# Moving the DRAM additions of a seven-product matmul: a pause under the first blocks of w_up, a denser run from the sixth block on

## The chip, the cores and the metric

One core of a Trainium2 chip runs the kernel. The metric is the device time of one execution in microseconds. Before the change three runs gave a median of 1739.53 us (1737.74 to 1740.78).

## What is computed

One decoder block on 256 tokens of width 2048, float32: a norm, one wide input projection, two branches (a gated linear recurrence and a dilated attention), their merge, and then a feed-forward part with a causal convolution of width 3. The change touches only how the weights of that feed-forward part are prepared:

```python
def conv_ffn(u, w_up, conv_w, conv_b, w_down):
    hup = u @ w_up                       # 2048 -> 2 x 5632
    hc = lax.conv_general_dilated(hup, ...) + conv_b
    a, b = hc[..., :D_FF], hc[..., D_FF:]
    return (jax.nn.gelu(a) * b) @ w_down
...
h = h + conv_ffn(rmsnorm(h, norm2_g[l]), w_up[l], conv_w[l], conv_b[l], w_down[l])
```

## The kernel before, in words

All weights are streamed once, in the order in which TensorE needs them, as 300 units of 1 MB (128 partitions x 2048 floats). `load(u)` (line 290) brings a unit into one of three `raw` slots, from SP's queue. `split(u)` turns each float into a high and a low part that TensorE can multiply fast: ScalarE (ACT) copies the high part (line 380 for plain units), VectorE (DVE) subtracts to get the low part (line 381). A product is then three matmuls.

Units 0 to 131 are the input projection, 132 to 167 the merge and output projections, 168 to 299 the feed-forward part. That part runs in 11 blocks `b`, each with 8 units of `w_up`, and from block 1 on two or four units of `w_down` behind them; from block 3 on a block is 12 units. The results of a `w_down` piece are evicted by ACT to a staging tile (`dns`, line 1078) and added to `h` by an accumulating DMA from POOL's queue (line 1079); ACT, DVE and TensorE meanwhile work off the convolution of the block before (`hidden_side`, line 1043: the transposes into `ua..t`, `ub..t` at line 1028, the taps `..e` at line 1036, from the same ring of staging tiles).

In most `w_up` units (mode "S", 60 of 88) TensorE does a 2 x 2 block product with seven products in place of eight. For that four sums of the unit's weight blocks are needed. Two of them, q1 (the first block plus the fourth) and q2 (q1 plus the third), are made in DRAM long before. `add_blocks` (line 255) makes one step of that: it copies a weight block into a DRAM tile (SP, 256 KB) and adds another to it with an accumulating DMA (POOL, line 267, 256 KB), which gives q1 of the next S unit; and for the unit three steps back it copies q1 to a second tile (SP, line 266) and adds the third block (POOL), which gives q2. So a full call issues two DMAs on SP and two on POOL; the last three calls of all find no new unit and issue one each. The SP copies are ordered behind the latest load of a whole unit (`in_turn(loaded[-1])`).

An S unit is then loaded as three transfers: 768 KB of weights (line 297), q1 behind them (line 298), and q2 into a tile of its own (line 300). `split_s` splits q2 (`sg`), the four blocks (`sa`, `se`), forms two more sums on DVE (lines 354, 355) and splits those (`sf`), all at lines 327 and 328. A plain unit is one transfer of 1 MB (line 303).

`begin_unit(u)` (line 414) is the clock of the whole: before the matmuls of unit `u` it splits units up to `u + 2`, loads unit `u + 3`, runs some side work, and then calls `add_blocks` until `additions(u)` calls have been made. `additions` (line 137) is the schedule that the change rewrites; 60 S units and three trailing steps make 63 calls.

Of the kernel before, what the change touches and what calls it, by code (L numbers as in the profile page):

```python
# [130 lines left out]
MODES = stream_spec()[1]  # L131

DRAM_SUMS = sorted(u for u, mode in MODES.items() if mode == "S")
ADD_FROM, ADD_TO, ADD_LATE = 44, 166, 8


def additions(u):
    n = len(DRAM_SUMS) + 3
    if u <= ADD_TO:
        return max(0, (u - ADD_FROM) * (n - 12) // (ADD_TO - ADD_FROM))  # L140
    return min(n, n - 12 + (u - ADD_TO) // ADD_LATE)

# [49 lines left out]
def hybrid_block(ctx, tc, x_p, x_t, weights, g1, gf, params, c_rope, c_mask0, c_mask1, c_level, out):  # L194
# [219 lines left out]
    def begin_unit(u):  # L414
        for v in range(u, u + LOOKAHEAD + 1):
            split(v)
        load(u + LOOKAHEAD + 1)
        pump(SIDE_US)
        while added[0] < additions(u):
            add_blocks()  # L420
            added[0] += 1
# [742 lines left out]
```

## Time and profile before

| | |
|---|---|
| median of 3 runs | 1739.53 us |
| the profiled execution's own time | 1738.46 us |
| its span | 1736.7 us |
| TensorE busy | 1713.5 us |
| DVE busy | 1301.3 us |
| ACT busy | 1053.7 us |
| granted TensorE clock, mean | 0.998 |

The span runs from the first to the last instruction. "Busy" is the time in which an engine had at least one instruction under way. A wait row names the engine and tile that waited and the one that released it. "DMA share" is the mean busy share of the core's 16 DMA engines. `up4v`, `ub3t` and so on are tiles of block 4 and block 3.

### The profile page before, as it was taken

To read this page: it belongs to the slowest core of one execution; us is meant where nothing else is said; L and a number is where in the kernel's file an instruction comes from. 1 tells how busy PE (TensorE), PEld (TensorE's weight loads), DVE (VectorE), ACT (ScalarE), POOL (GpSimd) and SP (SyncE) were. 2 spreads that over 40 slices of the span, in tenths; PEclk is the share of its full clock that TensorE was granted. 3 is DMA by queue.
4 is the path that set the end of the run, shared out by engine and by line. 5 is a ranking of instruction groups with operands and counts; after the bars stand their busy time and mean duration, and the time that the engine had idled before them with its cause. 6 is when DMAs were issued, how large, how long until landed. Compare 5 with 4: busy or idle time off the path is not lost. (4 is left out here: it accounts for less than half of the span.)

```text
span 1736.7 us, 22219 instructions
## 1 busy us (share of the span) xinstructions
PE 1713.5 (99%) x8292; PEld 1428.7 (82%) x8292; DVE 1301.3 (75%) x1559; ACT 1053.7 (61%) x1436; POOL 140.5 (8%) x181
## 2 busy tenths in 40 slices
PE   9999999999999999999999999999999999999998
PEld 8888888888888888888888887787777878888886
DVE  7765575776858675444656688999889889889886
ACT  6444465555455554544445568877776777887773
POOL 0000000011111011011111100110110110110000
PEclk9999999999999999999999999999999999999999
DMA  7765634778778787889998977887787788787672
GB/s 279 232 207 201 232 145 160 229 230 242 229 247 243 225 257 224 259 271 289 293 272 249 274 231 249 277 254 249 210 286 258 229 279 269 217 263 262 204 263 97
DMA packets 98684, 416.19 MB, mean 240 GB/s; under 512 B 11936, under 2 KB 12192, under 8 KB 67152
## 3 DMA queue, kind: packets, MB, share of 16 engines
q1 hardware_dynamic: 73344, 365.22, 58.5%
q0 software_dynamic: 23936, 46.15, 16.3%
q10 hardware_dynamic: 1296, 3.41, 0.5%
q8 instruction: 65, 1.06, 0.2%
q14 instruction: 43, 0.35, 0.1%
HBM read 400.05 MB, written 65.01 MB: 268 GB/s over the span
## 5 line engine op out<-in xcount | busy, mean ns | idle before, releaser
L380 ACT ACTIVATE hl<-raw 128x1024 fp32r<-128x1024 f32 (+1 forms) x480 | 500.9, 1055 | 502.1 <-PE egp L539 79.1
L381 DVE TENSOR_TENSOR hl<-raw,hl 128x1024 fp32r<-128x1024 f32 (+1 forms) x480 | 579.2, 1218 | 292.2 <-ACT hl L380 290.5
L267 POOL DMA_DIRECT2D q<-weights x120 | 99.7, 901 | 1113.3 <-DMA q<-q 821.3
L537 PE MATMUL dn<-hl,ff 128*128 128x512 f32 x320 | 126.7, 399 | 0.2 <-DVE up2c L621 0.2
L539 PE MATMUL dn<-hl,ff 128*128 128x512 f32 x320 | 125.0, 391 | 0.0
L538 PE MATMUL dn<-hl,ff 128*128 128x512 f32 x320 | 124.7, 390 | 0.0
L537 PE MATMUL egp<-hl,xu 128*128 128x512 f32 x256 | 100.5, 393 | 0.0
L539 PE MATMUL egp<-hl,xu 128*128 128x512 f32 x256 | 99.8, 390 | 0.0
L538 PE MATMUL egp<-hl,xu 128*128 128x512 f32 x256 | 99.7, 389 | 0.0
L328 DVE TENSOR_TENSOR se<-raw,se 128x1024 fp32r<-128x1024 f32 x60 | 73.2, 1221 | 16.6 <-ACT se L327 16.5
L327 ACT ACTIVATE sf<-raw 128x1024 fp32r<-128x1024 f32 x60 | 64.0, 1067 | 30.7 <-DVE raw L355 30.2
L328 DVE TENSOR_TENSOR sa<-raw,sa 128x1024 fp32r<-128x1024 f32 x60 | 73.2, 1220 | 9.8 <-ACT sa L327 9.8
L328 DVE TENSOR_TENSOR sf<-raw,sf 128x1024 fp32r<-128x1024 f32 x60 | 73.3, 1222 | 8.4 <-ACT sf L327 8.2
L327 ACT ACTIVATE se<-raw 128x1024 fp32r<-128x1024 f32 x60 | 63.9, 1066 | 25.1 <-PE up L600 12.6
L539 PEld LDWEIGHTS dn<-hl,ff 128*128 128x128 f32 x320 | 60.1, 188 | 13.1
L537 PEld LDWEIGHTS dn<-hl,ff 128*128 128x128 f32 x320 | 60.1, 188 | 12.7 <-DVE up2c L621 0.6
L538 PEld LDWEIGHTS dn<-hl,ff 128*128 128x128 f32 x320 | 60.2, 188 | 11.6
L327 ACT ACTIVATE sa<-raw 128x1024 fp32r<-128x1024 f32 x60 | 63.7, 1061 | 8.6 <-PE dn L539 4.9
L450 PE MATMUL ak<-xu,hl 128*128 128x512 f32 x192 | 67.1, 394 | 0.0
L539 PEld LDWEIGHTS egp<-hl,xu 128*128 128x128 f32 x256 | 48.1, 188 | 9.9
L538 PEld LDWEIGHTS egp<-hl,xu 128*128 128x128 f32 x256 | 48.1, 188 | 9.7
L537 PEld LDWEIGHTS egp<-hl,xu 128*128 128x128 f32 x256 | 48.1, 188 | 9.7
(585 smaller groups left out, 4417.6 us busy)
## 6 DMA issues: line engine op xcount, KB each, us to landing
raw<-weights SPq DMA_DIRECT2D x238, 1024.0 KB, 5.4
raw<-weights SPq DMA_DIRECT2D x60, 768.0 KB, 5.8
q<-weights POOLq DMA_DIRECT2D x120, 256.0 KB, 7.4
q<-q SPq DMA_DIRECT2D x120, 256.0 KB, 5.1
q<-weights SPq DMA_DIRECT2D x60, 256.0 KB, 6.3
raw<-q SPq DMA_DIRECT2D x60, 256.0 KB, 6.1
h<-dns POOLq DMA_DIRECT2D x36, 256.0 KB, 6.2
h<-x_t ACTq DMA_DIRECT2D x4, 512.0 KB, 6.6
```

What stands on the lines that cost most here:

```text
L267: nc.gpsimd.dma_start(q, weights[u, :, i * 512 : (i + 1) * 512], accum_op=ALU.add)
L327: act.activation(hi, src, AF.Copy)
L328: vec.tensor_tensor(lo, src, hi.bitcast(F32), op=ALU.subtract)
L380: last[0] = act.activation(hi[:, q * w : (q + 1) * w], raw, AF.Copy)
L381: last[1] = vec.tensor_tensor(lo[:, q * w : (q + 1) * w], raw, hi[:, q * w : (q + 1) * w].bitcast(F32), op=ALU.subtract)
L450: pe.matmul(ps, hi, pair, start=(k == 0), stop=False, skip_group_check=True)
L537: pe.matmul(pst[m], xl, hi, start=(k == k0), stop=False)
L538: pe.matmul(pst[m], xh, hi, start=False, stop=False)
L539: pe.matmul(pst[m], xh, lo, start=False, stop=(k == k0 + nk - 1))
```

## The change

The number of calls made by the time a unit begins is spread differently. Before, 51 of the 63 calls are made evenly over units 44 to 166, and the other 12 one every eight units, at units 174, 182, ..., 262. After, 50 are made by unit 166, none in units 167 to 219, and the other 13 one every four units, at units 220, 224, ..., 268. Unit 168 is the first of `w_up` block 0, unit 220 the first of block 5, unit 268 the first of block 9. Nothing else is changed.

```diff
 DRAM_SUMS = sorted(u for u, mode in MODES.items() if mode == "S")
-ADD_FROM, ADD_TO, ADD_LATE = 44, 166, 8
+ADD_FROM, ADD_TO = 44, 166
+ADD_AGAIN, ADD_LATE, LAST_ADDS = 216, 4, 13
 
 
 def additions(u):
     n = len(DRAM_SUMS) + 3
     if u <= ADD_TO:
-        return max(0, (u - ADD_FROM) * (n - 12) // (ADD_TO - ADD_FROM))
-    return min(n, n - 12 + (u - ADD_TO) // ADD_LATE)
+        return max(0, (u - ADD_FROM) * (n - LAST_ADDS) // (ADD_TO - ADD_FROM))
+    return min(n, n - LAST_ADDS + max(0, (u - ADD_AGAIN) // ADD_LATE))
```

## Rows read from the trace of the kernel before

**Rows 1.** The page: the span, and TensorE's busy time.
```profile
span 1736.7 us, 22219 instructions
...
PE 1713.5 (99%) x8292; PEld 1428.7 (82%) x8292; DVE 1301.3 (75%) x1559; ACT 1053.7 (61%) x1436; POOL 140.5 (8%) x181
```

**Rows 2.** Stretches: start:end, length, busy (instructions) per engine, clock, DMA share, GB/s.
```profile
40.00:1040.00 1000.00, 999.88 (x5081) 847.08 (x5081) 655.66 (x805) 512.13 (x639) 89.61 (x114) 1.00 0.76 236
1040.00:1266.56 226.56, 218.34 (x979) 176.00 (x978) 204.21 (x237) 174.61 (x260) 18.81 (x22) 1.00 0.78 251
1266.56:1333.27 66.71, 64.37 (x288) 51.79 (x287) 57.94 (x67) 48.61 (x72) 6.97 (x8) 1.00 0.83 259
1333.27:1398.23 64.96, 63.69 (x288) 52.06 (x287) 58.05 (x67) 49.16 (x72) 5.21 (x6) 1.00 0.80 251
1398.23:1462.06 63.83, 63.08 (x285) 51.23 (x284) 57.88 (x67) 48.95 (x73) 6.09 (x7) 1.00 0.83 264
1462.06:1525.52 63.46, 63.46 (x288) 52.15 (x287) 57.96 (x67) 49.34 (x73) 4.36 (x5) 1.00 0.77 249
1588.95:1651.91 62.96, 62.96 (x285) 51.79 (x284) 57.47 (x66) 48.74 (x72) 3.50 (x4) 1.00 0.71 236
```

**Rows 3.** Waits of PE, 1040 to 1266.56 us: total, times, longest.
```profile
PE ub3t L1028 <- ACT ub3e L1036: 3.2, 1, 3.2
PE up L598 <- DVE up0v L610: 1.5, 1, 1.5
PE ua1t L1028 <- ACT ua1e L1036: 0.9, 1, 0.9
```

**Rows 4.** Waits of PE, 1266.56 to 1462.06 us.
```profile
PE up L600 <- DVE sf L328: 3.7, 4, 1.6
PE ub5t L1028 <- ACT ub5e L1036: 0.6, 1, 0.6
```

**Rows 5.** Timeline of SP's issues, 1290 to 1345 us: start, length, line, what.
```profile
1293.61 0.33 SPq L303 DMA_DIRECT2D raw<-weights  x1
1293.99 0.47 SPq L266 DMA_DIRECT2D q<-q  x1
1294.52 0.59 SPq L266 DMA_DIRECT2D q<-weights  x1
1301.67 0.34 SPq L297 DMA_DIRECT2D raw<-weights  x1
...
1324.68 0.33 SPq L303 DMA_DIRECT2D raw<-weights  x1
...
1334.05 4.33 SPq L303 DMA_DIRECT2D raw<-weights  x3
...
1343.27 0.47 SPq L266 DMA_DIRECT2D q<-q  x1
```

**Rows 6.** The chain that ended last, 1200 to 1240 and 1290 to 1330 us.
```profile
1220.10 14.66 DMA h<-dns
...
1303.36 11.77 DMA q<-q
```

**Rows 7.** Timeline of ACT and of DVE, 1300 to 1340 us.
```profile
1315.21 0.63 ACT L327 ACTIVATE sg<-q 128x512 fp32r<-128x512 f32 x1 [4.54 <-DMA q<-q]
...
1315.88 0.69 DVE L328 TENSOR_TENSOR sg<-q,sg 128x512 fp32r<-128x512 f32 x1 [3.00 <-ACT sg L327]
```

**Rows 8.** Stretches of the projections, columns as in rows 2.
```profile
200.00:320.00 120.00, 119.88 (x651) 102.18 (x651) 76.03 (x113) 71.12 (x101) 1.72 (x2) 1.00 0.50 174
720.00:960.00 240.00, 240.00 (x1078) 198.02 (x1077) 132.02 (x137) 106.69 (x118) 29.71 (x36) 1.00 0.91 276
```

**Rows 9.** Tile q: count, shortest/median/longest ns, first and last start.
```profile
L267 POOL DMA_DIRECT2D q<-weights x120: 807/818/1527, 291.4 to 1532.6; - x120
L266 SPq DMA_DIRECT2D q<-weights x60: 496/582/1340, 285.9 to 1400.0; - x60
L266 SPq DMA_DIRECT2D q<-q x60: 473/473/490, 328.1 to 1526.7; - x60
```

## Prediction

> **What bounds the kernel now.** The page comes first: TensorE (PE) is busy 1713.5 of 1736.7 us [rows 1], so no rearrangement that leaves its matmuls alone can win more than 23 us, and what can be won is only time in which PE waits. The next view is the busy time by stretches [rows 2]. In the 1000 us from 40 to 1040, which hold 51 of the 63 calls of `add_blocks` (by the formula, up to unit 166) and most of the projections, PE is idle 0.12 us: the calls cost nothing there. From 1040 to 1266.56 (most of block 0, blocks 1 to 3, and w_up of block 4) it is idle 226.56 - 218.34 = 8.22 us. After that I cut the stretches at the end of the w_up phase of blocks 4, 5, 6, 7, 8 (the start of `up4t`, `up5t`, ...), so each is one block's work, 12 units. With one half call (a copy and an accumulation; the last three calls have no new block to add) a period takes 63.46 us and PE never waits; I take that as the floor. The others take 66.71, 64.96 and 63.83 us, so 3.25, 1.50 and 0.37 over it. POOL's instruction count tells how many calls each holds, since 4 of its instructions are the accumulations into `h` and a full call adds 2: the period of 66.71 us has two full calls, that of 64.96 one, that of 63.83 one and a half. Together 8.22 + 5.12 = 13.3 us are at stake, 0.8% of the span. The rest of PE's idle time lies at the two ends of the kernel.
>
> What the waits are is read from who released PE [rows 3, 4]. Nearly all are waits for a split or a tap, so for DVE or ACT, and DVE is busy 57.96 of 63.46 us in the undisturbed period [rows 2]: it has 5.5 us to spare per block. A late load takes from that spare time. One call can be followed whole. SP issues its two copies at 1293.99 and 1294.52, right behind the load of unit 3 of w_up block 5 [rows 5]. The q2 that an S unit needs then lands after 11.77 us [rows 6]; ACT waits 4.54 us for it, and DVE 3.00 us for ACT [rows 7]. DVE then works without a gap and PE still catches up with it: most of the 3.7 us waited for `sf` [rows 4]. A second pattern is the 3.2 us before `ub3t` [rows 3]: an accumulation into `h` that landed after 14.66 us [rows 6] held the staging tile that the tap needed.
>
> **What the change does, part by part.** *Units 44 to 166*: 50 calls instead of 51. Cover: a stretch where calls cost 0.12 us at most [rows 2]. I take nothing; if the calls' new places broke that cover, one late load would cost what a call costs below.
>
> *Blocks 0 to 4 (units 168 to 219)*: the calls of units 174, 182, 190, 198, 206 and 214 go. Each takes with it two SP issues of 0.47 and 0.58 us, two POOL issues of 0.82 us [rows 9], and four transfers of 256 KB. What those occupy of the 16 DMA engines is read from two stretches of projections with the same loads [rows 8]: with one call in 120 us (POOL x2) their share is 0.50, with 18 calls in 240 us (x36) 0.91; 218 - 120 = 98 us for the 16 calls by which they differ from two stretches of the first kind, 6.1 us a call. The periods give less: 0.83 x 66.71 - 0.71 x 62.96 = 10.7 us for two calls, 5.3 each; 7.3 for one; 8.3 for one and a half [rows 2]. I take 5.5. Of the 8.22 us of idle time I keep the 1.5 us at `up0v`, where DVE is behind from the start of the stage, and 0.6 us of the small ones. Gain: 6.1 us (bounds: 8.2, all of it, and 4.1, only `ub3t` and `ua1t`, which follow a call directly).
>
> *Blocks 5 to 9*: calls 51 to 63 come at units 220, 224, ..., 268, so at unit 0 and unit 4 of w_up and at unit 0 of w_down of each block. On SP a call stands behind the latest whole load, which is that of three units on; so they fall behind the loads of up unit 3 (1293.61 in rows 5), up unit 7 (1324.68) and down unit 3 (the last of the three from 1334.05). By the same rule today's calls of units 222 and 230 stand behind up unit 3 and down unit 3, at 1293.99 and 1343.27 [rows 5]. Two of the three new places therefore have a price in this trace. Down unit 3: the period with that call alone lost 1.50. Up unit 3: the period of 3.25 has it and a call behind down unit 1; charging the latter the 0.37 of the period that has it with a half call, 2.9 remain. Up unit 7 has none: between 0 (DMA is slack there) and 2.9 (as up unit 3); I take the 0.37 of down unit 1, the load two units on. Three calls a block cost 4.7 us. As issue time a call takes 1.05 us of SP and 1.64 of POOL. On SP that is covered: behind the call of 1294.52 the next load goes out at 1301.67 [rows 5], when a slot comes free; without that cover 1.05 us a call, 11 in all, would be late. On POOL the accumulations into `h` queue behind it; what that costs is in the measured periods already.
>
> Sum: period 4 to 5 (units 220, 224) 3.2; 5 to 6 and 6 to 7 (three calls each) 4.7 each; 7 to 8 (units 252, 256, a half call at 260) 1.5 + 2.9 + 0 = 4.4; 8 to 9 (half calls at 264 and 268) 0, as the period of 63.46. That is 17.0 in place of 5.1, so 11.9 lost and 6.1 gained: **5.8 us slower**. As a cross-check, DMA would be occupied 44.7 + 3 x 5.5 = 61 us of each 63.5: nearly always, where today's worst period has 55 of 66.7. No block's addition arrives late: the last copy is called at unit 268, and unit 286, which reads it, is loaded at 283, some 15 units of 5.3 us later.
>
> The profiled execution took 1738.46 us, 1.8 more than its span, and the median of the runs is 1739.53; the difference is added to the median: 1745.3.
>
> **Rivals.** *The calls are absorbed, and the gain stays* (faster). For it: the period of 63.83 lost 0.37 with one and a half calls, and PE waits for nothing once only half calls run. Against: those calls are half as large or stand where DVE has spare time, and both places I priced high are kept. It decides if a call delays DVE by under 5.5 / 3 = 1.8 us; the one that I followed delayed it by 3.0. At 0.25 us a call, 11.5 calls cost 2.9: 2.9 - 5.1 - 6.1 = -8.3, 1731.2 us. The Trainium skill ("DMA: Bandwidth & Descriptors", Anatomy of one DMA — SWDGE (gpsimd) path) fits a transfer as about 2.0 us fixed plus its bytes over 436 GB/s; by that an estimated 2.4 us of engine time for a call's four, 52 us of DMA a period, and this rival. The 5.3 to 7.3 us that the rows give for a call speak against it.
>
> *Each call costs the same wherever it stands.* Today's 11.2 us (6.1 + 5.1) over nine full and three half calls, 10.5 in all, are 1.07 each; the new plan has 11.5 calls: +1.1 us, 1740.6. For it: what is lost is spread over blocks 1 to 6. Against: 0.37 and 2.9 for calls of one size.
>
> *The accumulations into h are caught as well* (slower still): three calls a block leave no quiet gap for them, and the 3.2 us at `ub3t` come back in the three blocks with most calls: 9.6 on top, 1754.9. Against: it happened at full size once in seven blocks.
>
> That the change has no effect is excluded: the issues on SP follow the formula's units.
>
> **How the numbers follow.** About 0.2%, 3.5 us, is what a measurement of this kernel can tell from no change. Forecast 0.46 (0.41 slower by more, 0.05 within); same price everywhere 0.22 (0.20 within, 0.02 slower); absorbed 0.24 (0.22 faster, 0.02 within); accumulations caught 0.08 (slower). Faster 0.22, same 0.27, slower 0.51. The bounds of the gain move the forecast by 2 either way, up unit 7 at 2.9 instead of 0.37 adds 2.5 x 3 = 7.6, at 0 it takes 1.1. The range must reach the centre of the absorbed case, and on the other side the forecast with up unit 7 dear: 1730 to 1754.
>
> **What would show it.** Right: PE idle from 1040 to the end of block 3 falls to about 2 us, and the periods of blocks 5 to 8 are 66 to 69 us with DMA shares of 0.9 and more and waits of PE for `sf`. Wrong: those periods stay near 63.5 us (absorbed), or PE's waits in blocks 0 to 3 remain without calls, which would mean that DVE alone made them.

## The result, and the profile after

The changed kernel takes 1748.53 us (median of 14 runs, 1741.87 to 1754.63), the kernel before in the same sessions 1737.72 us (14 runs). The ratio is 1.006 with a 95% interval of 1.0048 to 1.0073: **slower by 0.5 to 0.7%**. The medians differ by 10.8 us; the two profiled executions, whose rows are compared here, by 9.8 us (spans of 1746.5 and 1736.7 us). The forecast was 5.8 us slower.

In the changed kernel every line number is one higher. The first view is that of the stretches, with the cuts at the same events as in [rows 2] (`up3t`, `up4t`, ..., here at 1195.98, 1260.58, ... us).

```profile
40.00:1040.00 1000.00, 999.87 (x5077) 846.29 (x5076) 654.50 (x804) 510.99 (x638) 88.01 (x112) 1.00 0.76 235
1040.00:1195.98 155.98, 153.02 (x692) 124.19 (x691) 144.95 (x169) 125.27 (x190) 7.02 (x8) 1.00 0.70 231
1195.98:1260.58 64.60, 63.98 (x290) 52.50 (x289) 59.99 (x70) 50.06 (x73) 3.51 (x4) 1.00 0.73 242
1260.58:1324.73 64.15, 63.93 (x288) 52.22 (x287) 57.49 (x66) 48.66 (x71) 7.01 (x8) 1.00 0.78 247
1324.73:1394.11 69.38, 65.67 (x287) 53.17 (x286) 58.30 (x67) 49.41 (x72) 8.62 (x10) 0.98 0.86 269
1394.11:1463.65 69.54, 65.59 (x287) 53.15 (x287) 58.32 (x67) 49.28 (x72) 8.65 (x10) 0.98 0.86 265
1463.65:1530.87 67.22, 64.37 (x290) 52.45 (x289) 58.67 (x68) 49.93 (x74) 7.81 (x9) 1.00 0.89 279
1530.87:1598.50 67.63, 64.62 (x285) 52.61 (x284) 57.95 (x67) 49.38 (x73) 5.23 (x6) 0.97 0.80 247
1598.50:1661.41 62.91, 62.91 (x285) 51.79 (x284) 57.45 (x66) 48.69 (x71) 3.51 (x4) 1.00 0.72 236
```

The pause pays: the end of block 4's w_up comes at 1260.58 instead of 1266.56 us, 6.0 us earlier, and the period from there to `up5t` takes 64.15 instead of 66.71, another 2.6. PE is idle 3.6 us from 1040 to there (2.96 and 0.62) where it was 8.2 [rows 2]. Then the next four periods take 69.38, 69.54, 67.22 and 67.63 us, in place of 64.96, 63.83, 63.46 and 63.43 (the last from 1525.52 to 1588.95 us): 18.1 us more. The period after them is again free.

The two free periods of the kernel before, 63.46 and 63.43 us, give a floor of 63.44. Of the 20.0 us by which the four periods exceed it, PE is idle 13.5 (69.38 - 65.67 and so on). The largest waits of PE, in three stretches parted by dots: 1040 to 1280, 1280 to 1460 and 1460 to 1640 us:

```profile
PE up L599 <- DVE up0v L611: 1.7, 1, 1.7
PE ub2t L1029 <- ACT ua2e L1037: 1.2, 1, 1.2
...
PE dn L538 <- DVE up6c L622: 2.9, 1, 2.9
PE up L601 <- DVE sf L329: 2.5, 5, 0.7
PE dn L538 <- DVE up5c L622: 2.4, 1, 2.4
...
PE dn L538 <- DVE up8c L622: 2.3, 1, 2.3
PE dn L538 <- DVE up7c L622: 2.2, 1, 2.2
PE up L601 <- DVE sf L329: 1.4, 2, 0.7
```

`ub3t` and `ua1t` of [rows 3] are gone. In place of them stands a wait that the kernel before had only once, at 0.2 us: the first w_down unit of a block (`dn`) waits 2.2 to 2.9 us, once in each of blocks 5 to 8, 9.8 us in all. At the end of a block's w_up phase `unfold` combines the seven sums in PSUM into the block's four results (`up6c` and so on); call that the unfolding. Its two steps at lines 621 and 622 (in the changed kernel's numbers) read the same PSUM bank; the first w_down product reuses it for its second half of the tokens. Why line 622 comes late is shown by the chain that ended last, from 1380 to 1412 us (block 6):

```profile
1395.41 9.25 DMA raw<-weights
...
1404.74 1.07 ACT hl L381
...
1408.91 0.79 PE dn L538
```

The load of the second w_down unit takes 9.25 us. DVE's timeline from 1396 to 1412 us shows what that does:

```profile
1402.37 0.75 DVE L621 SCALAR_TENSOR_TENSOR up6c<-up,rstd_r,up6c 128x512 f32<-128x512 f32 x1
1405.84 2.36 DVE L382 TENSOR_TENSOR hl<-raw,hl 128x1024 fp32r<-128x1024 f32 x2 [2.71 <-ACT hl L381]
1408.11 0.74 DVE L622 SCALAR_TENSOR_TENSOR up6c<-up,rstd_r,up6c 128x512 f32<-128x512 f32 x1
```

The split of that unit (`hl`) stands between lines 621 and 622 on DVE. DVE is idle 2.71 us for it and runs line 622 only behind it, and the bank is held meanwhile. That a split stands ahead of these steps is not new. In the kernel before (block 5, one line number less) the split of the same unit stands ahead of both, but its load takes 4.75 us and DVE does not wait:

```profile
1334.05 4.75 DMA raw<-weights
...
1339.98 2.36 DVE L381 TENSOR_TENSOR hl<-raw,hl 128x1024 fp32r<-128x1024 f32 x2
```

What fills the DMA engines then is seen in SP's timeline from 1384 to 1416 us:

```profile
1386.04 0.33 SPq L304 DMA_DIRECT2D raw<-weights  x1
1386.42 0.47 SPq L267 DMA_DIRECT2D q<-q  x1
...
1390.20 0.34 SPq L304 DMA_DIRECT2D raw<-weights  x1
...
1395.41 4.69 SPq L304 DMA_DIRECT2D raw<-weights  x3
1400.20 0.47 SPq L267 DMA_DIRECT2D q<-q  x1
```

The call of up unit 4 (1386.42) falls behind the load of up unit 7, as the prediction placed it, right ahead of the w_down loads. Two theories were then open. **Place**: that one call, beside the w_down loads, does the harm. **Amount**: with three calls a block the DMA engines are full, wherever the calls stand.

### The profile page after: what moved, and what is told of

It is laid out like the page before. It is cut to its first block, busy times and chain, and to the rows that moved or that the text cites. A ratio compares the mean times of both kernels' runs of the same rounds, so it can differ in the third digit from the quotient of the medians.

```text
span 1746.5 us, 22207 instructions
## 1 busy us (share of the span) xinstructions
PE 1718.2 (98%) x8292; PEld 1432.4 (82%) x8292; DVE 1301.8 (75%) x1559; ACT 1054.1 (60%) x1436; POOL 141.0 (8%) x181
## 4 chain that ended last, share of the span: by engine, by line
PE 76%; issue 10%; DVE 6%; DMA 5%; ACT 2%; SPq 0%; POOL 0%; DVEq 0%; ACTq 0%; POOLq 0%
PE dn L538 3%; PE dn L540 3%; PE egp L538 3%; PE egp L540 3%; PE dn L539 3%; PE egp L539 3%; PE up L601 3%; PE up L599 3%; PE up L600 3%; DMA raw<-weights 3%; PE ak L451 3%; DMA q<-q 2%; PE aq L451 2%; PE gp L538 2%; PE gp L540 2%
## 5 line engine op out<-in xcount | busy, mean ns | idle before, releaser
L538 PE MATMUL dn<-hl,ff 128*128 128x512 f32 x320 | 129.4, 405 | 9.8 <-DVE up6c L622 2.9
L540 PE MATMUL dn<-hl,ff 128*128 128x512 f32 x320 | 126.7, 396 | 0.0
L539 PE MATMUL dn<-hl,ff 128*128 128x512 f32 x320 | 126.5, 395 | 0.0
L1080 POOL DMA_DIRECT2D h<-dns x36 | 36.8, 1081 | 353.1 <-ACT dns L1079 345.9
L540 PEld LDWEIGHTS egp<-hl,xu 128*128 128x128 f32 x256 | 48.1, 188 | 10.0
L539 PEld LDWEIGHTS egp<-hl,xu 128*128 128x128 f32 x256 | 48.1, 188 | 9.7
```

The costliest lines, as they stand in the source:

```text
L538: pe.matmul(pst[m], xl, hi, start=(k == k0), stop=False)
L539: pe.matmul(pst[m], xh, hi, start=False, stop=False)
L540: pe.matmul(pst[m], xh, lo, start=False, stop=(k == k0 + nk - 1))
```

## The experiments

Each was timed 5 to 12 times beside the kernel before, in three sessions: e1 to e4, e5 to e8, and e9 to e12. The kernel before took 1737.85, 1738.64 and 1737.33 us in them, so a difference of times from two sessions can be off by about 1 us.

**e1: the same thirteen calls, two units earlier.**

```diff
-ADD_AGAIN, ADD_LATE, LAST_ADDS = 216, 4, 13
+ADD_AGAIN, ADD_LATE, LAST_ADDS = 214, 4, 13
```

> The thirteen late calls stay four units apart but come two units earlier: at units 218, 222, ..., 266, so at up units 2 and 6 and at down unit 2 of a block, never at up unit 4. Theory of the place: what costs is the call at up unit 4, whose transfers run beside the loads of the first w_down units; DVE then stands at their split ahead of the unfolding, and the first w_down matmul waits 2.2 to 2.9 us for its PSUM bank. Then those waits of dn for up5c to up8c are gone, and about 3 us for each of four blocks with them: 1735 to 1741 us. Theory of the amount: the DMA engines are over 0.85 busy with three calls a block wherever they stand, and a call costs some 1.8 us anywhere: 1746 to 1751 us, as the changed kernel.

Measured: 1729.96 us, ratio 0.9961 (0.9949 to 0.9973), faster than the kernel before and 18.6 us faster than the changed one. Its periods from `up4t` to `up8t`:

```profile
1259.57:1324.16 64.59, 64.59 (x291) 52.62 (x290) 58.04 (x67) 49.15 (x72) 7.03 (x8) 1.00 0.86 269
1324.16:1388.72 64.56, 63.67 (x287) 51.77 (x286) 57.97 (x67) 48.66 (x73) 8.65 (x10) 1.00 0.91 285
1388.72:1452.92 64.20, 63.30 (x286) 51.48 (x285) 57.78 (x67) 48.64 (x72) 8.65 (x10) 1.00 0.91 286
1452.92:1516.60 63.68, 63.68 (x288) 51.95 (x287) 57.89 (x67) 49.02 (x72) 7.76 (x9) 1.00 0.88 282
```

POOL's counts (x10) are those of the changed kernel, the DMA share is higher (0.91), and a period loses 0.2 to 1.1 us. The theory of the amount falls. The theory of the place had the sign right and was still too careful by 5 us.

**e2: the call at up unit 4 moved to down unit 2, the others left.**

```diff
-    return min(n, n - LAST_ADDS + max(0, (u - ADD_AGAIN) // ADD_LATE))
+    return min(n, n - LAST_ADDS + sum(v <= u and (v - 220) % 12 in (0, 8, 10) for v in range(220, 270)))
```

> Thirteen late calls again, three a block, at up unit 0 and at down units 0 and 2 (units 220, 228, 230, 232, 240, ..., 268): the call at up unit 4 is moved to down unit 2, the others stay. Theory of the place: no wait of dn for up6c to up8c, 1734 to 1741 us. Theory of the amount: 1746 to 1751 us, and more if three calls in 25 us crowd each other.

Measured: 1731.01 us, ratio 0.9965 (0.9952 to 0.9978), 17.5 us under the changed kernel, with its calls at up unit 0 and down unit 0 unchanged. Of the waits of dn for the unfolding one of four is left, in PE's waits of 1040 to 1700 us:

```profile
PE dn L538 <- DVE up6c L622: 1.6, 1, 1.6
```

So the expectation that they vanish held for all but one; the time was 3 us better than expected. In e1 and e2 the order that the scheduler gives DVE's instructions changed too: one pair of `hl`, which the changed kernel has ahead of the first step of the unfolding, is back behind it, as in the kernel before. So these two runs alone do not part the transfers from that order; e7 does so further down.

**e3 and e4: no late calls, and the pause alone.** e3 sets `ADD_FROM, ADD_TO` to 16, 166 and `LAST_ADDS` to 0; e4 sets the second line to 214, 8, 6.

> All 63 calls are made by unit 166, from unit 16 on, at the rate per unit that the kernel before has (0.42); no call is left under w_up. Both theories: PE waits only at up0v and for about 1 us more under w_up, and every period from block 3 on takes about 63.5 us, so that 10 to 12 us of the kernel before are gained: 1726 to 1730 us. If a part of the waits in blocks 0 to 4 is DVE's own, the gain is less. If the calls from unit 16 on disturb the start of the projections, PE would show waits between 80 and 300 us.

> The pause alone: 57 calls by unit 166 in place of 51, from unit 44 on as before, and the last six at units 222, 230, ..., 262 as in the kernel before. Both theories: the 6 to 8.5 us of blocks 0 to 4 are gained and nothing is paid in blocks 5 to 9: 1729 to 1732 us. If the projections, with DMA engines busy 0.91 between 720 and 960 us, can't take 12 per cent more calls, PE waits appear there.

Measured: e3 1734.59 us, ratio 0.998 (0.9969 to 0.9991); e4 1729.61 us, ratio 0.9959 (0.9943 to 0.9975). e4 met its expectation: the pause is worth about 8 us. e3 missed its own by 5 us. Under w_up it is as quiet as expected (periods of 63.44 us); it lost the time earlier, in PE's waits of 40 to 1040 us:

```profile
PE avp L540 <- DVE hl L382: 4.9, 2, 4.6
```

The wait of 4.6 us stands at 210 us, under the attention projections, and the granted clock is 0.50 in the 2 us behind it. That the early calls made it is not shown by itself; e5, with no call before unit 44, lacks it.

**e5: all 63 calls between units 44 and 166.**

```diff
-ADD_AGAIN, ADD_LATE, LAST_ADDS = 216, 4, 13
+ADD_AGAIN, ADD_LATE, LAST_ADDS = 216, 4, 0
```

> All 63 calls between units 44 and 166, none later: the start of e4 and the quiet w_up of e3 together. Both theories: the 2.5 us that e4 still lost between up4t and up6t are gained and nothing is lost at the start: 1726 to 1728 us. If 0.52 calls a unit are too many for the projections, PE waits show between 300 and 1040 us and it is slower than e4.

Measured: 1726.71 us, ratio 0.9928 (0.9916 to 0.9941): as expected, and **the best version found**, 12 us under the kernel before. The projections take the denser calls (DMA share 0.80 from 40 to 1040 us, where it was 0.76) with 0.12 us of idle PE.

```profile
40.00:1040.00 1000.00, 999.88 (x5076) 846.41 (x5075) 654.42 (x803) 510.81 (x637) 106.74 (x135) 1.00 0.80 247
...
1323.33:1386.78 63.45, 63.45 (x288) 52.19 (x287) 57.95 (x67) 49.20 (x73) 3.51 (x4) 1.00 0.73 241
```

Its w_up periods are at the floor, so a call can be priced on it alone. Six of the next seven experiments add calls of no use to it, which add two blocks each into DRAM tiles that nothing reads.

**e6 and e7: four extra calls at up unit 4, full and without their accumulations.**

```diff
+EXTRA = tuple(220 + 12 * i + 4 for i in range(4))
...
+    def extra_call(u):
+        for i in (0, 2):
+            q = dram.tile([P, 512], F32, tag=f"x{i}_{u}", name=f"x{i}_{u}")
+            with in_turn(loaded[-1]):
+                nc.sync.dma_start(q, weights[u, :, 3 * 512 :])
+            nc.gpsimd.dma_start(q, weights[u, :, i * 512 : (i + 1) * 512], accum_op=ALU.add)
...
+        if u in EXTRA:
+            extra_call(u)
```

> e5 and four calls of no use at units 224, 236, 248 and 260, up unit 4 of blocks 5 to 8: each two copies on SP and two accumulations on POOL into DRAM tiles that nobody reads. Theory of the place, the call alone: each costs 4 to 5 us, with a wait of the first w_down matmul of 2 to 3 us: 16 to 20 us over e5. Rival, crowding: the call at up unit 4 hurts only because that at down unit 0 follows it 14 us later on SP and the DMA engines stay full; alone it costs under 1 us: less than 4 us over e5.

> As e6 but the extra calls have their two copies on SP only, no accumulation. If the accumulations hold back the w_down loads: under 4 us over e5, half of e6's loss or less. If it is the copies in SP's order ahead of the loads, or the order that the scheduler gives DVE once the call stands there: as e6.

Measured: e6 1736.21 us (0.9978 to 0.9999), 9.5 us over e5, 2.4 us a call: between the two theories. e7, without the last line of `extra_call`, 1730.69 us (0.994 to 0.9965), 4.0 over e5, 1.0 a call; its interval just touches that of e5. The waits of dn after 1040 us, first in e6 and then in e7 (the unfolding's line 622 is 633 and 632 there):

```profile
PE dn L549 <- DVE up7c L633: 2.4, 1, 2.4
PE dn L549 <- DVE up6c L633: 2.3, 1, 2.3
...
PE dn L549 <- DVE up8c L633: 1.8, 1, 1.8
...
PE dn L549 <- DVE up5c L633: 1.2, 1, 1.2
```

```profile
PE dn L548 <- DVE up7c L632: 1.5, 1, 1.5
...
PE dn L548 <- DVE up8c L632: 0.4, 1, 0.4
PE dn L548 <- DVE up5c L632: 0.4, 1, 0.4
```

A call at up unit 4 alone makes the new wait in every one of the four blocks. More than half of it is due to the accumulations: 9.5 against 4.0 us, 7.7 against 2.3 us of waits. In both kernels the scheduler puts one more pair of `hl` ahead of the first step of the unfolding on DVE, as in the changed kernel. With that order alike, the accumulations make the difference of 5.5 us. Whether the 4.0 us that e7 still costs are due to its copies or to that order was not tried.

**e8: the changed kernel, with the second w_down unit's split behind the unfolding.**

```diff
         for v in range(u, u + LOOKAHEAD + 1):
+            if u >= 220 and (u - 220) % 12 == 7 and v == u + 2:
+                continue
             split(v)
```

> The changed kernel with its calls where they are, but from block 5 on the split of the second w_down unit is asked for at the first w_down unit and not two units ahead, so that on DVE it stands behind the whole unfolding and no longer ahead of its fifth step (line 622). Theory of the place by DVE's order: the first w_down matmul no longer waits for up5c to up8c, and 3 us or more per block come back: 1733 to 1740 us. Rival, the late load hits PE anyway: the wait moves to the second w_down unit (dn for hl) and it stays at 1744 us or more.

Measured: 1736.2 us, ratio 0.9983 (0.9972 to 0.9993), 12.3 us under the changed kernel, inside the range of the first theory. But the waits have not vanished, as it had said: dn still waits for blocks 5 to 8, 6.2 us in all in place of 9.8 (the line is 624 there).

```profile
PE dn L540 <- DVE up7c L624: 2.7, 1, 2.7
PE dn L540 <- DVE up8c L624: 1.7, 1, 1.7
```

In its profiled execution (1739.5 us, 3.3 over the median) three of the four periods are 2.2 to 4.7 us shorter than in the changed kernel. The one with the wait of 2.7 us is 3.8 us longer, with a granted clock of 0.50 behind that wait from 1466 to 1472 us:

```profile
1453.66:1524.64 70.98, 68.03 (x293) 55.02 (x292) 58.66 (x68) 49.93 (x74) 8.60 (x10) 0.95 0.84 265
```

So the place of that split on DVE carries the larger part of the loss by the medians. The split of the first w_down unit still stands ahead of the unfolding and may make the rest; that is not shown by a run of its own.

**e9 to e11: four such calls at up unit 2, up unit 0 and down unit 0.** `EXTRA` as in e6 with 2, 0 and 8 in place of 4.

> e5 and four extra full calls as in e6, at up unit 2 of blocks 5 to 8 (units 222, 234, 246, 258), where the kernel before and e1 have calls. Theory of the place: little, under 1 us a call, 1727 to 1731 us. By the price that the prediction took for a call behind the load of up unit 3, 2.9 us each: 1738 us.

> The same four extra calls at up unit 0 (units 220, 232, 244, 256), behind the load of up unit 3 too. Theory of the place: under 1 us a call, 1727 to 1731 us. By the prediction's 2.9 us: 1738 us.

> The same four extra calls at down unit 0 (units 228, 240, 252, 264). Theory of the place: under 1 us a call, 1727 to 1731 us; the prediction's 1.5 us give 1733 us.

Measured: e9 1731.58 us (0.9954 to 0.9979) and e10 1732.0 us (0.9955 to 0.998), 4.9 and 5.3 over e5, so 1.2 and 1.3 a call, a little over what the theory of the place gave and half or less of the prediction's price. e11 1726.35 us (0.9927 to 0.9954): no cost that can be measured. e5 was timed in another session; by the ratios to the kernel before, the costs are 1.7, 1.7 and 0.5 a call, and e11's interval still overlaps that of e5. Two of e11's periods with a call (POOL x6):

```profile
1322.64:1386.14 63.50, 63.50 (x287) 52.09 (x286) 57.89 (x67) 49.30 (x72) 5.17 (x6) 1.00 0.79 256
1386.14:1449.54 63.40, 63.40 (x288) 52.18 (x287) 57.89 (x67) 49.21 (x73) 5.17 (x6) 1.00 0.80 257
```

The waits of e9 are those for `sf`, as in [rows 4], and none of dn (1200 to 1700 us):

```profile
PE up L612 <- DVE sf L338: 4.0, 6, 0.9
```

**e12: extra calls at up unit 4 and at down unit 0 together.** `EXTRA` with 4 and 8.

> Eight extra calls, at up unit 4 and down unit 0 of blocks 5 to 8, so that two follow each other closely as in the changed kernel. If the prices add: what e6 and e11 lose over e5 together, some 10 to 13 us, 1736 to 1740 us. If the two crowd each other, as the changed kernel's 17 us over e2 for the same number of calls suggest: 15 us or more, 1742 us and up.

Measured: 1737.83 us, ratio 1.0004 (0.9993 to 1.0015), 11.1 us over e5, some 13 by the ratios. The prices add (9.5 and -0.4, or 10.6 and 2.1 by the ratios), and these two calls do not crowd each other measurably.

## Why the prediction was right, and which terms were off

**The sign and the bound.** Slower was the likeliest case, and 1748.53 lies in the range. The account of what bounds the kernel held in its main line: PE waits for DVE, and DVE for a late load. The wait itself was another than forecast. The prediction looked for waits for `sf`; they are 3.9 us in blocks 5 to 8, the waits of `dn` for the unfolding 9.8. It had no term for a split that stands on DVE ahead of the step that frees a PSUM bank. Of its other signs, the periods came out nearly as said (67.2 to 69.5 for 66 to 69 us), the DMA shares did not (0.80 to 0.89 for 0.9 and more), and PE's idle time up to the end of block 3's w_up fell to 3.0 us, not to 2.

**Luck in the size.** For the three periods from `up5t` to `up8t` 13.8 us were forecast and 15.8 measured, because two places taken too dear made up for one taken far too cheap. Where they could not, the sum was off: `up4t` to `up5t` 0.7 for 3.2, `up8t` to `up9t` 4.2 for nothing. In all 20.7 us for 17.0.

**Blocks 0 to 4.** Gain forecast 6.1 us, measured 6.0 at `up4t`; `up0v` stayed at 1.7 (1.5 before), as kept. The period after `up4t` gained 2.6 more (64.15 for 66.71), and e4 shows the pause alone to be worth 8 us.

**The projections.** Taken at nothing, and so it is: 999.87 of 1000 us busy.

**Up unit 7's load, the term that failed.** The prediction charged the call behind it 0.37 us and named 2.9 as the upper bound. Alone it costs 2.4 us (e6). In the changed kernel, moving just these calls gains 17.5 us (e2), which is 4.4 to 5.0 us each for three full calls and a half one, as the half one is counted. It runs beside the loads that DVE must split ahead of the unfolding's last steps, and those hold PSUM banks that the next products need. The harm shows after the end of w_up, so the price of the call of unit 224 falls in the period after the one that it was charged to.

**Up unit 3's and down unit 3's loads.** 2.9 and 1.5 us were taken; added to e5 they cost 1.2 to 1.3 (e9, e10) and nothing (e11). The prices had been read off whole periods, in which waits from before the call also lie. These are waits of PE in the kernel before, in the timelines of 1300 to 1345 us:

```profile
1324.71 0.50 PE L600 MATMUL up<-sf,hvx 128*128 128x512 f32 x1 [1.58 <-DVE sf L328]
1335.21 0.50 PE L600 MATMUL up<-sf,hvx 128*128 128x512 f32 x1 [0.67 <-DVE sf L328]
```

Behind the call that the prediction followed, at 1293.99 us, PE waited 1.58 us. That is not most of the 3.7 us of [rows 4], and about half of the 2.9. The wait of 0.67 us lies in the period that gave down unit 3 its 1.5 us, but ahead of that call, which is issued at 1343.27.

**The half calls.** The period of `up8t` to `up9t` was charged nothing, by the row in which a half call is free [rows 2]. It lost 4.2 us, about as much as the periods with full calls. The product that waits in it is that of block 8, behind the half call of unit 260, again up unit 4.

**The cross-check by DMA share** argued nothing. The changed kernel's share is 0.80 to 0.89 as its four periods lose 3.8 to 6.1 us; e1 has 0.91 and loses 1.

**The rivals.** That the calls are absorbed is nearly what happens with three calls a block in other places (e1, e2), and its time of 1731.2 us lies beside theirs. Its engine time for a call is not borne out: e11's four periods with a call have shares of 0.79 to 0.81 where e5's have 0.73, which is 0.06 to 0.08 of 63.45, so 3.8 to 5.1 us a call. The estimate of 2.4 us was worked out from the Trainium skill ("DMA: Bandwidth & Descriptors", Anatomy of one DMA — SWDGE (gpsimd) path). That each call costs the same everywhere falls by e6 and e11 (2.4 us and nothing measurable). That the accumulations into `h` are caught did not happen: no wait for a tap is left in the list from 1280 to 1640 us.

**Still open**: why the call at up unit 4 costs about twice as much in the changed kernel as alone. It is not the call at down unit 0 (e12). The halved clock below may be a part of it: it follows three of the four waits in the changed kernel's trace, and one of four in e6's. The call at up unit 0 beside both was not tried.

## What to carry to other kernels

In this kernel, which is bound by TensorE, background transfers were priced by what they delay, not by how full the DMA engines are: the same thirteen calls gave 1748.5 and 1730.0 us two units apart. Look for the spot where an engine has a split of a just-loaded tile ahead of the instruction that frees a PSUM bank, and keep extra transfers away from the loads that feed it. And if another stage has slack enough for all of them, as the projections have here, put them there (e5).

## What was not expected of the hardware

After three of the four waits of dn, TensorE ran at half its clock for some 3 us. Stretches of the changed kernel, block 5 (the wait ends at 1339.03 us) and, below the dots, block 7 (1477.67 us):

```profile
1338.00:1340.00 2.00, 0.97 (x4) 0.83 (x5) 2.00 (x4) 1.30 (x2) 0.00 (x0) 1.00 0.98 330
1340.00:1342.00 2.00, 2.00 (x7) 1.56 (x7) 2.00 (x3) 1.06 (x1) 1.18 (x2) 0.62 0.84 287
1342.00:1344.00 2.00, 2.00 (x9) 1.60 (x8) 1.70 (x2) 0.59 (x1) 0.47 (x1) 0.52 1.02 269
...
1478.00:1480.00 2.00, 2.00 (x10) 1.65 (x9) 2.00 (x4) 0.58 (x1) 0.45 (x1) 1.00 0.78 268
```

The granted clock falls to 0.52, the lower of its two levels, 1.2 GHz, and matmuls that stood 0.227 us apart stand 0.427 apart. In the changed kernel it did so after waits of 2.44, 2.94 and 2.30 us, but not after one of 2.16, nor after the 3.2 us of [rows 3] in the kernel before, where the clock stayed at 1.00. In e12 it fell after waits of 2.12 and 1.98 us, in e6 after one of 2.41 and not after one of 2.25. So the length of the wait alone does not tell. PE counts as busy meanwhile.

Of the 20.0 us that the four periods lose, 6.5 are not idle time of PE. Three such stretches of some 3 us at 0.427 in place of 0.227 us a matmul are, as an estimate, some 4.5 us of it; that share was not measured by itself. The period from `up7t` to `up8t`, with a clock of 1.00, has 0.9 of the 6.5 too.
